# A two-layer encoder: u and v of the mixer as one Strassen product, its last part inside the attention, the engines' order written out

## The chip, the cores and the metric

The kernel runs on one core of one Trainium2 chip. The metric is the device time of one execution in microseconds (us). TensorE (PE) multiplies matrices, VectorE (DVE) and ScalarE (ACT) prepare and finish its operands, GpSimd (POOL) and SyncE (SP) issue transfers.

## What is computed

The input is 512 tokens of 1024 channels, on a grid of 8 rows by 64 columns. Two layers follow each other; then comes a last RMSNorm.

```python
def reference(...):
    for l in range(L):
        x = x + 0.5 * swiglu(rms_norm(x, ffn1_norm[l]), ffn1_w_in[l], ffn1_w_out[l])
        x = x + mixer(rms_norm(x, mix_norm[l]), mix_w_in[l], ...)
        x = x + 0.5 * swiglu(rms_norm(x, ffn2_norm[l]), ffn2_w_in[l], ffn2_w_out[l])
    return rms_norm(x, final_norm)

def mixer(h, w_in, gate_bias, rpb, w_na_out, w_f_out, w_o):
    z = h @ w_in                    # q, k, v, uf: 512 columns each; ga, gf: 1024 each
    y_na = neighbourhood_attention(q, k, v, rpb) @ w_na_out   # 8 heads of 64
    y_f = fourier_mix(uf) @ w_f_out # real part of a 2-D DFT over positions and 128 channels, 4 groups
    return (sigmoid(ga + gate_bias[0]) * y_na + sigmoid(gf + gate_bias[1]) * y_f) @ w_o
```

The change touches the mixer: how v and uf ("u" in the kernel) are computed, and in which order the rest of the mixer stands around that.

## The kernel before

**Numbers in two parts.** Each operand of a product is split into a high part (`fp32r`, made on ACT by a copy) and a low part (the difference, made on DVE). `mm3` (L285 to L288) and `late_low` (L446 to L450) then issue three matmuls: high by high, high by low, low by high. A weight "granule" is 128 by 1024; `Item.prep` makes its `whi` on ACT (L175, or L170 when negated) and its `wlo` on DVE (L178, L171), three buffers of each. `Item.summed` (L160) adds two granules on DVE where a product needs a sum of weights.

**Products in seven parts.** The feed-forward products, the two gates and the last product of the mixer use Strassen's scheme: `product` issues one part of 24 matmuls of 128x512 (four blocks of the inner dimension, two blocks of rows, three matmuls), and seven parts in place of eight give the four quadrants. Sums of activations (the tiles `t1` to `t3`) and of weights go in, `snap` (L517) copies a result out of PSUM, `less` (L522) subtracts. Where `strassen` is called with `dma=True`, sums of weights are made by transfers that accumulate, issued on POOL's queue (L146).

**The mixer's order.** `proj_U` computes u without such a scheme, together with a mirrored copy from activations that `mirrored` (L986, L987) reverses; `proj_V` computes v. Both take all eight blocks of the inner dimension in three matmuls each. After u comes `norm.rstd()`, the reciprocal root on DVE (L304 to L309), and `norm.spread(R)`, which writes it to DRAM and reads it back as a row for all partitions (`row<-r`, `R<-row`, on POOL's queue). Then:

```python
        u = proj_U()
        vt = proj_V()
        bias_for(0)
        ...
        for g in range(4):
            four_pos(g)
        proj_q(0)
        proj_k(0)
        for g in range(4):
            four_ch(g)
        proj_q(1)
```

`four_pos` transforms over positions and rotates, `four_ch` over channels; each of the four groups leaves a pair `y` that `rows_of` multiplies with the Fourier weights later (`fill`). `proj_T` makes one pair of heads of q or k: 24 matmuls, a product with `R` (L970), high and low. `att_scores` (L1104), `att_probs` (maxima with the bias on DVE L1118, exponentials on ACT L1124, reciprocals L1127, scalings on ACT L1131), `att_trans` (transposes on PE L1140, then `p` high and low) and `att_out` follow per pair of blocks; `att_next(hp)` transposes the two blocks of one pair of heads and scores the next two. PSUM has eight banks, handed out in rotation; `slot` has 23 buffers, `tmp` eight.

A scheduler orders the instructions on each engine by priority. Inside `tc.manual_schedule(engines=...)` the named engines keep the order of the program text; before the change this is used at a few places only, none of them in the first part of the mixer.

## Time and profile before

| | |
|---|---|
| median of 3 runs | 1905.67 us (1904.82 to 1905.99) |
| the profiled execution | 1906.04 us, of which its span is 1904.2 |
| granted TensorE clock | 0.999 |
| layer 0's mixer, first product | from 337 us |
| layer 0's gates, first product | from 492 us |

A row of the profile's groups reads: line, engine, operation, output tile <- input tiles, shapes, count | busy us, mean ns of one | idle time of the engine before them and what ended it. In the table of windows each engine has its busy time and count, then come the granted clock, the share of the transfers and GB/s. In the timeline and the chain the first number is the start and the second the length, both in us.

### The profile page before, as it was taken

What the parts mean: (1) busy time and instruction counts of PE and PEld (TensorE: products, weight loads), DVE (VectorE), ACT (ScalarE), POOL (GpSimd) and SP (SyncE); (2) the same over time, 40 slices, a digit from 0 to 9 for tenths busy, and PEclk for the clock granted to TensorE, in tenths of its full rate; (3) what the DMA queues carried; (4) which work ended last, traced back from release to release, by engine and by line L of the source; (5) the groups of instructions that cost most, each with busy time, mean ns of one, the idle gap of its engine ahead of it and who ended that gap; (6) DMA issues with size and microseconds to landing.
All of it is one profiled execution on the core that took longest, in us unless ns stands there. A gap on an engine that the chain in (4) does not pass through costs nothing.

```text
span 1904.2 us, 25091 instructions
## 1 busy us (share of the span) xinstructions
PE 1891.7 (99%) x9189; PEld 1586.8 (83%) x9189; DVE 1602.4 (84%) x2000; ACT 1161.6 (61%) x1676; POOL 160.7 (8%) x198
## 2 busy tenths in 40 slices
PE   9999999999999999999999999999999999999998
PEld 7888888888888888888888888888888888888886
DVE  7877899586889987889997778995769899787899
ACT  6655665468566755566665556663675576555655
POOL 0101010000111010001010100100001101000010
PEclk9999999999999999999999999999999999999999
DMA  8776499323886776649877664992247867766594
GB/s 301 202 207 187 150 249 320 105 84 104 217 218 166 180 195 204 177 152 262 251 185 210 187 180 152 268 339 74 68 130 215 215 170 175 207 177 177 170 275 147
DMA packets 104636, 364.36 MB, mean 191 GB/s; under 512 B 12032, under 2 KB 12160, under 8 KB 104512
## 3 DMA queue, kind: packets, MB, share of 16 engines
q1 hardware_dynamic: 77568, 270.70, 40.1%
q0 software_dynamic: 26800, 92.04, 26.8%
q8 instruction: 72, 1.18, 0.2%
q14 instruction: 52, 0.43, 0.1%
q10 hardware_dynamic: 144, 0.02, 0.0%
HBM read 357.46 MB, written 2.11 MB: 189 GB/s over the span
## 4 chain that ended last, share of the span: by engine, by line
PE 95%; issue 2%; DMA 2%; DVE 1%; ACT 0%; POOL 0%; DVEq 0%; ACTq 0%; POOLq 0%; SPq 0%
PE A L447 9%; PE A L448 9%; PE A L450 9%; PE o L448 7%; PE o L447 7%; PE o L450 7%; PE ps L286 5%; PE ps L288 5%; PE ps L287 5%; PE B L448 4%; PE B L447 4%; PE B L450 4%; PE C L448 2%; PE C L447 2%; PE C L450 2%; PE tr L540 2%
## 5 line engine op out<-in xcount | busy, mean ns | idle before, releaser
L175 ACT ACTIVATE whi<-raw 128x1024 fp32r<-128x1024 f32 (+1 forms) x528 | 546.1, 1037 | 423.4 <-PE A L448 123.2
L178 DVE TENSOR_TENSOR wlo<-raw,whi 128x1024 fp32r<-128x1024 f32 (+1 forms) x528 | 627.3, 1193 | 191.2 <-ACT whi L175 186.5
L146 POOL DMA_DIRECT2D raw<-in_wst_dram x158 | 136.2, 873 | 1440.2 <-DMA raw<-in_wst_dram 674.7
L160 DVE TENSOR_TENSOR raw<-raw,raw 128x1024 f32<-128x1024 f32 (+1 forms) x146 | 172.6, 1191 | 1.2
L448 PE MATMUL A<-whi,xl 128*128 128x512 f32 x384 | 149.5, 389 | 0.0
L447 PE MATMUL A<-whi,xh 128*128 128x512 f32 x384 | 149.4, 389 | 0.0
L450 PE MATMUL A<-wlo,xh 128*128 128x512 f32 x384 | 110.5, 389 | 0.0
L170 ACT ACTIVATE whi<-raw 128x1024 fp32r<-128x1024 f32 (+1 forms) x79 | 81.6, 1036 | 40.2 <-PE A L448 12.4
L171 DVE SCALAR_TENSOR_TENSOR wlo<-raw,whi 128x1024 fp32r<-128x1024 f32 (+1 forms) x79 | 93.1, 1193 | 12.2 <-ACT whi L170 12.2
L633 ACT ACTIVATE th<-sn,rh 128x512 f32<-128x512 f32 x80 | 56.8, 714 | 69.4 <-DVE sn L522 69.4
L517 ACT ACTIVATE sn<-A 128x512 f32<-128x512 f32 x96 | 56.4, 589 | 51.3 <-PE A L450 51.2
L450 PEld LDWEIGHTS A<-wlo,xh 128*128 128x128 f32 x384 | 72.1, 188 | 15.0
L448 PEld LDWEIGHTS A<-whi,xl 128*128 128x128 f32 x384 | 72.1, 188 | 14.8
L447 PEld LDWEIGHTS A<-whi,xh 128*128 128x128 f32 x384 | 72.1, 188 | 14.8
L447 PE MATMUL B<-whi,t1h 128*128 128x512 f32 x192 | 76.2, 397 | 0.0
L447 PE MATMUL A<-whi,t3h 128*128 128x512 f32 x192 | 75.3, 392 | 0.4 <-ACT sn L517 0.4
L447 PE MATMUL C<-whi,xh 128*128 128x512 f32 x192 | 74.9, 390 | 0.0
L447 PE MATMUL A<-whi,t2h 128*128 128x512 f32 x192 | 74.9, 390 | 0.0
L448 PE MATMUL B<-whi,t1l 128*128 128x512 f32 x192 | 74.8, 390 | 0.0
L448 PE MATMUL A<-whi,t3l 128*128 128x512 f32 x192 | 74.8, 390 | 0.0
L448 PE MATMUL C<-whi,xl 128*128 128x512 f32 x192 | 74.7, 389 | 0.0
L448 PE MATMUL A<-whi,t2l 128*128 128x512 f32 x192 | 74.7, 389 | 0.0
(409 smaller groups left out, 4748.2 us busy)
## 6 DMA issues: line engine op xcount, KB each, us to landing
raw<-in_wst_dram SPq DMA_DIRECT2D x466, 512.0 KB, 5.4
raw<-in_wst_dram POOLq DMA_DIRECT2D x162, 512.0 KB, 7.9
raw<-in_wst_dram SPq DMA_DIRECT2D x30, 256.0 KB, 3.9
bm<-in_bias_dram SPq DMA_DIRECT2D x16, 384.0 KB, 6.0
vs<-v SPq DMA_DIRECT2D x12, 256.0 KB, 4.9
x<-in_xin_dram SPq DMA_DIRECT2D x4, 512.0 KB, 10.2
raw<-in_wst_dram POOLq DMA_DIRECT2D x8, 256.0 KB, 8.7
dft<-in_dft_dram POOLq DMA_DIRECT2D x8, 256.0 KB, 6.2
```

The costliest lines, as they stand in the source:

```text
L146: G.dma_start(out=self.t, in_=wst[GRAN_AT[self.plus]][:, 0 : self.n], accum_op=ALU.add)
L160: V.tensor_tensor(self.raw.t, self.raw.t, self.add.t, ALU.add)
L170: S.activation(hi, t, AF.Copy, scale=-1.0)
L171: self.last = V.scalar_tensor_tensor(lo, t, -1.0, hi.bitcast(F32), ALU.mult, ALU.subtract)
L175: S.activation(hi[:, cs], t[:, cs], AF.Copy)
L178: self.last = V.tensor_tensor(lo[:, cs], t[:, cs], hi[:, cs].bitcast(F32), ALU.subtract)
L286: PE.matmul(ps, lh, rh, start=start, stop=False, skip_group_check=again)
L287: PE.matmul(ps, lh, rl, start=False, stop=False, skip_group_check=again)
L288: PE.matmul(ps, ll, rh, start=False, stop=stop, skip_group_check=again)
L447: PE.matmul(ps, lh, rh, start=start, stop=False, skip_group_check=again)
L448: PE.matmul(ps, ll, rh, start=False, stop=False, skip_group_check=again)
L450: PE.matmul(ps, lh, rl, start=False, stop=stop, skip_group_check=again)
```

## The change

- **u and v are one product** (`proj_UV`). Their weights form a block matrix, u's beside v's, and it is multiplied in seven parts, in the order 1, 5, 6, 2, 3, 7, 4. Projections of q and k stand between the parts: their granules come in the weights' order behind the fifth, sixth, second, third and seventh part. u is complete behind part 3. Part 4 is issued behind the first scores.
- **The mirrored u** comes from the finished u: `turn` multiplies its high and low part by a reversed identity (`mir`), four matmuls, inside the second k projection. `flip` now holds the small product that reverses the reciprocal roots.
- **Activations**: the mixer's normalised x is copied raw, then split once per quarter (`quad_high`: 1024 columns high, 1024 low), as its sums (`combos`, shared with the feed-forward stage) are taken from the raw copy. The reciprocal root uses ACT's square root (`rstd_steps`), so ACT loads the table of the square root in the feed-forward stage before, and that of the exponential in the mixer.
- **Fourier stage in two halves**: groups 0 and 1, then 2 and 3 inside the attention. `four_pos`, `four_ch` and `att_probs` are cut into steps (`rotated`, `four_q`, `four_y`, `four_high`; class `Probs` with `maxes`, `exps`, `inverse`, `scaled`; `att_pv`, `att_split`), `proj_T` into the product, high and low.
- **Order written out** for PE, DVE and ACT, from the mixer's start to the scores of the third pair of heads. `tmp` has 11 buffers. The first block of rows of the Fourier product (`pf`) moves there too. In `fill` of `o`, the first two blocks start with three of their four inner blocks.

The core of the diff (cut; lines of the old `proj_U`, `proj_V` and of the plain loop over heads are left out):

```diff
+                for key in (behind or {}).get(m, ()):
+                    add(Raw(key))
...
-            for name, n in (("u", 4), ("v", 4), ("qk", 8), ("f", 4)):
-                for g in range(n):
-                    add(Raw((s, name, g)))
+            qk = [(s, "qk", g) for g in range(8)]
+            strassen(s, lambda q: "u" + q, 0, two, (1, 5, 6, 2, 3, 7, 4), True, behind={5: qk[0:1], 6: qk[1:2], 2: qk[2:3], 3: qk[3:4], 7: qk[4:5]})
+            for key in qk[5:] + [(s, "f", g) for g in range(4)]:
+                add(Raw(key))
...
+        def quad_high(self, i, j):
...
+            S.activation(hq, raw, AF.Copy)
+            return lambda: V.tensor_tensor(lq, raw, hq.bitcast(F32), ALU.subtract)
...
+        def rstd_steps(self):
+            ms, q, t = small("ms", 4), small("sq", 4), small("rt", 4)
+            r = self.r = small("r", 4)
+            V.tensor_tensor(ms, self.ssq[:, 0:4], self.ssq[:, 4:8], ALU.add)
+            V.tensor_scalar(ms, ms, 1.0 / D, EPS, ALU.mult, ALU.add)
+            S.activation(q, ms, AF.Sqrt)
+            yield
+            V.reciprocal(r, q)
+            V.tensor_tensor(t, r, r, ALU.mult)
+            V.scalar_tensor_tensor(t, t, -0.5, ms, ALU.mult, ALU.mult)
+            V.scalar_tensor_tensor(r, t, 1.5, r, ALU.add, ALU.mult)
+            yield
...
+        def combine(m):
+            p, a, b, op = {
+                5: ((0, 0), (0, 0), (0, 1), ALU.subtract),
+                7: ((0, 1), (0, 1), (1, 1), ALU.subtract),
+                6: ((0, 0), (1, 1), (0, 0), ALU.add),
+                4: ((1, 0), (1, 0), (0, 0), ALU.subtract),
+            }[m]
+            V.tensor_tensor(raw[p], raw[a], raw[b], op)
+            yield
+            if m != 4 or not t4:
+                acts[m] = (slot(F32R, f"t{m}h"), slot(F32R, f"t{m}l"), 0)
+            h, l, _ = acts[m]
+            S.activation(h, raw[p], AF.Copy)
+            yield
+            V.tensor_tensor(l, raw[p], h.bitcast(F32), ALU.subtract)
+            yield
+        return acts, combine
...
-            return mp.tile([P, T], dt, tag="tmp", name=nm(s), bufs=8)
+            return mp.tile([P, T], dt, tag="tmp", name=nm(s), bufs=11)
...
+        def proj_UV():
+            acts, combine = combos(norm, None)
+            ws.depth = 8
+            steps = {m: combine(m) for m in (5, 6, 7, 4)}
+            def step(m, n=1):
+                for _ in range(n):
+                    next(steps[m])
+            step(5)
+            def t1():
+                step(5, 2)
+                norm.squares(1, 0)
+            pa = pair("A")
+            product(pa, acts[1], K4, True, hook=t1)
+            root = norm.rstd_steps()
+            next(root)
+            ws.items[ws.prepped + 1].summed()
+            next(root)
+            norm.spread(R)
+            ws.prep(ws.pos + 3)
+            low10 = norm.quad_high(*norm.due.pop(0))
+            s1 = snap(pa)
+            norm.low01()
+            step(6, 2)
+            pb = pair("B")
+            product(pb, acts[5], K4, True, hook=low10)
+            sb = snap(pb)
+            S.activation(small("sq", 1), ones, AF.Exp)
+            step(6)
+            q0 = proj_T(DH**-0.5)
+            step(7, 2)
+            product(pa, acts[6], K4, False, again=True, hook=lambda: step(7))
+            s2 = snap(pa)
+            k0 = proj_T(None)
+            step(4, 2)
+            q0 = q0()
+            step(4)
+            pc = pair("C")
+            product(pc, acts[2], K4, True)
+            q[0] = q0()
+            q1 = proj_T(DH**-0.5)
+            k0 = k0()
+            less(pc, s1)
+            k[0] = k0()
+            product(pb, acts[3], K4, False, again=True)
+            q1 = q1()
+            less(pb, s2)
+            uh, ul = slot(F32R, "uh", (2, T)), slot(F32R, "ul", (2, T))
+            S.activation(uh, s2, AF.Copy)
+            q[1] = q1()
+            norm.flip()
+            V.tensor_tensor(ul, s2, uh.bitcast(F32), ALU.subtract)
+            S.activation(mir, mirror, AF.Copy)
+            flipped = []
+            def turn():
                 for c in range(2):
+                    pm = bank()
+                    PE.matmul(pm, mir, uh[:, 1 - c, :], start=True, stop=False)
+                    PE.matmul(pm, mir, ul[:, 1 - c, :], start=False, stop=True)
+                    t = tmp(s="uf")
+                    S.activation(t, pm, AF.Copy, scale=norm.rflip[:, c : c + 1])
+                    flipped.append(t)
+            k1 = proj_T(None, hook=turn)
             constants()
+            us, ue = [[], []], []
             for c in range(2):
                 for op in (ALU.add, ALU.subtract):
                     w = tmp(s="ue")
+                    V.scalar_tensor_tensor(w, s1[:, c, :], norm.r[:, c : c + 1], flipped[c], ALU.mult, op)
+                    ue.append(high_of(w, "u"))
+                    us[c].append(None)
+            for i, low_of in enumerate(ue):
+                us[i // 2][i % 2] = low_of()
+            product(pa, acts[7], K4, False, again=True, ahead=0)
+            ws.depth = FETCH
+            return us, k1, pa, sb, acts[4]
...
+        with tc.manual_schedule(engines={mybir.EngineType.DVE, mybir.EngineType.Activation}):
+            with tc.manual_schedule(engines={mybir.EngineType.PE}):
+                u, k1, pa, sb, acts4 = proj_UV()
+                fp = [four_pos(0), four_pos(1)]
+                bias_for(0)
+                k1 = k1()
+                ws.prep(ws.pos + 2)
+                bt = [rotated(fp[0])]
+                bh = [high_of(bt[0], "b")]
+                bt.append(rotated(fp[1]))
+                bh.append(high_of(bt[1], "b"))
+                less(pa, sb)
+                for c in range(2):
+                    v_high(2 + c, sb[:, c, :])
+                k[1] = k1()
+                b_ = [bh[0](), bh[1]()]
+                q2 = proj_T(DH**-0.5)
+                q2 = q2()
+                p0, p1 = [Probs(i, att_scores(i)) for i in range(2)]
+                p0.maxes(0)
+                p0.maxes(1)
+                p0.exps(0)
+                p1.maxes(0)
+                p0.inverse(0)
+                p0.exps(1)
+                p1.maxes(1)
+                p0.inverse(1)
+                p1.exps(0)
+                product(pa, acts4, K4, False, again=True, ahead=0)
+                ws.prep(ws.pos + 1)
+                q[2] = q2()
+                for c in range(2):
+                    v_high(c, pa[c])
+                f0, f1 = four_ch(b_[0]), four_ch(b_[1])
+                g0, g1 = four_q(f0[1]), four_q(f1[1])
+                for c in range(4):
+                    v_low(c, sb[:, c - 2, :] if c > 1 else pa[c])
+                vs = []
+                for s in range(3):
+                    t = slot(F32R, "vs", (2, T))
+                    nc.sync.dma_start(out=t[0:64].bitcast(F32), in_=vt[s][64:128].bitcast(F32))
+                    nc.sync.dma_start(out=t[64:128].bitcast(F32), in_=vt[s + 1][0:64].bitcast(F32))
+                    vs.append(t)
+                bias_for(1)
+                p1.exps(1)
+                fp = [four_pos(2), four_pos(3)]
+                y0 = four_y(f0[0], g0)
+                p1.inverse(0)
+                y1 = four_y(f1[0], g1)
+                p1.inverse(1)
+                ws.prep(ws.pos + 2)
+                k2 = proj_T(None, 1)
+                y0 = four_high(y0)
+                y1 = four_high(y1)
+                p0.scaled(0)
+                p0.scaled(1)
+                bt = [rotated(fp[0])]
+                bh = [high_of(bt[0], "b")]
+                p1.scaled(0)
+                bt.append(rotated(fp[1]))
+                bh.append(high_of(bt[1], "b"))
+                p1.scaled(1)
+                b_ = [bh[0](), bh[1]()]
+                k2 = k2()
+                ws.prep(ws.pos + 2)
+                fq = []
+
+                def second():
+                    fq.extend([four_ch(b_[0]), four_ch(b_[1])])
+
+                q3 = proj_T(DH**-0.5, 0, hook=second)
+                (f0, f1) = fq
+                g0, g1 = four_q(f0[1]), four_q(f1[1])
+                w0 = four_y(f0[0], g0)
+                w1 = four_y(f1[0], g1)
+                w0 = four_high(w0)
+                w1 = four_high(w1)
+                yf += [y0(), y1()]
+                q3 = q3()
+                ts = transposed(p0.s) + transposed(p1.s)
+                ph = [high_of(t, "p") for t in ts]
+                ph = [h() for h in ph]
+                pt_ = {0: ph[0:2], 1: ph[2:4]}
+                p2, p3 = [Probs(i, att_scores(i)) for i in (2, 3)]
+                k3 = proj_T(None, 0)
+                p2.maxes(0)
+                p2.maxes(1)
+                ws.prep(ws.pos + 1)
+                p2.exps(0)
+                p2.exps(1)
+                p3.maxes(0)
+                p2.inverse(0)
+                p3.maxes(1)
+                p2.inverse(1)
+                yf += [w0(), w1()]
+                p2.scaled(0)
+                p2.scaled(1)
+                p3.exps(0)
+                ws.prep(ws.pos + 2)
+                p3.exps(1)
+                k[2] = k2()
+                q[3] = q3()
+                p3.inverse(0)
+                k3 = k3()
+                p3.inverse(1)
+                bias_for(2)
+                vch = {i: (t[:, 0, :], t[:, 1, :]) for i, t in ((0, vt[0]), (1, vs[0]), (2, vt[1]), (3, vs[1]), (4, vt[2]), (5, vs[2]), (6, vt[3]))}
+                o.append(hilo("o"))
+                po = [att_pv(i, pt_.pop(i)) for i in range(2)]
+                first_f.extend([ws.next(0), ws.next(0)])
+                pf = rows_of(yf, 0, first_f)
+                att_split(0, po[0])
+                p3.scaled(0)
+                p3.scaled(1)
+                ts = transposed(p2.s) + transposed(p3.s)
+                k[3] = k3()
+                ph = [high_of(t, "p") for t in ts[0:2]]
+                pt_[2] = [h() for h in ph]
+                att_split(1, po[1])
+                ph = [high_of(t, "p") for t in ts[2:4]]
+                pt_[3] = [h() for h in ph]
+                ps = [att_scores(i) for i in (4, 5)]
+        sc = {i: att_probs(i, z) for i, z in zip((4, 5), ps)}
```

320 lines of the change are left out of this document (150 added, 170 removed).

## The prediction

> **What bounds the kernel now.** I read the page's busy times first, then TensorE's waits, the chain of work that ended last, and the windows over layer 0's mixer (337 to 500 us).
>
> ```profile
> span 1904.2 us, 25091 instructions
> PE 1891.7 (99%) x9189; PEld 1586.8 (83%) x9189; DVE 1602.4 (84%) x2000; ACT 1161.6 (61%) x1676; POOL 160.7 (8%) x198
> ...
> PE ps L132 <- ACT warm L129: 2.7, 1, 2.7
> PE A L447 <- ACT sn L517: 0.4, 2, 0.2
> ```
>
> TensorE (PE) is bound by its own work: in 1904.2 us it waits 3.1 us, 2.7 of them for the warm-up. So a matmul taken away is worth its pitch, as long as everything that feeds PE arrives in time. The pitch is in the chain (start, length, instructions) and in the timeline:
>
> ```profile
> 340.55 0.68 PE ps L288 x3
> 342.60 0.87 PE tr L364 x8
> 382.19 0.12 PE ps L286
> 421.23 1.69 PE L1104 MATMUL ps<-q,q 64*128 64x256 f32 x24
> ```
>
> A 128x512 matmul costs 0.68/3 = 0.227 us, a 128x128 transpose 0.109, a 256-wide matmul of the Fourier stage 0.12, a score matmul on 64 rows (they run in pairs) 1.69/24 = 0.07. (The mean of one, 0.39 us, overlaps its neighbours.)
>
> ```profile
> 337.00:359.60 22.60, 22.60 (x105) 18.82 (x104) 10.96 (x32) 8.70 (x18) 4.55 (x8) 1.00 0.41 134
> 359.60:381.40 21.80, 21.80 (x98) 18.07 (x98) 10.96 (x15) 9.50 (x13) 0.00 (x0) 1.00 0.06 21
> 381.40:400.00 18.60, 18.60 (x112) 16.63 (x112) 16.83 (x30) 8.00 (x12) 0.00 (x0) 1.00 0.53 142
> 400.00:420.00 20.00, 20.00 (x114) 16.69 (x113) 14.81 (x47) 14.46 (x37) 0.00 (x0) 1.00 0.21 67
> 420.00:440.00 20.00, 20.00 (x146) 17.56 (x146) 15.33 (x39) 16.15 (x42) 0.00 (x0) 1.00 0.13 40
> 440.00:460.00 20.00, 20.00 (x128) 17.19 (x125) 13.93 (x49) 15.15 (x44) 0.00 (x0) 1.00 0.15 54
> ```
>
> The columns are PE, weight loads, VectorE (DVE), ScalarE (ACT), POOL, the granted clock (1.00 throughout) and DMA. While u and v are projected, DVE is half idle (10.96 of 22.60); in the attention both feeders have a quarter to a third in reserve (13.93 to 15.33 and 14.46 to 16.15 of 20). That reserve is what this change spends.
>
> **What it removes and adds on PE.**
>
> ```profile
> L286 PE MATMUL ps<-whi,xh 128*128 128x512 f32 x96 | 37.7, 393 | 0.0
> L286 PE MATMUL ps<-whi,flip 128*128 128x512 f32 x32 | 12.4, 389 | 0.0
> ```
>
> u and v are one of three such rows each: 3 x (96 + 32) = 384 matmuls in two layers. Seven parts of 24 are 168 a layer, 336; the mirror of u adds 4 a layer. Net 384 - 336 - 8 = 40 fewer, 40 x 0.227 = **-9.1 us**, or 4.5 a layer. Attention, projections, Fourier and gates keep their counts. Were PE as dense as now, that would be the result: 1906.0 - 9.1 = 1896.9 for a profiled run.
>
> **What it adds on the feeders.** Counting instructions in the two orders, DVE gains, over both layers, 42 operations of 1024 columns (12 weight lows, 4 sums of weights, 8 combinations of activations with their 8 lows, 10 lows of x and u) and twelve subtractions of 512; it loses 32 small lows and 16 flips. By the rows below, and 0.62 us for 512 columns (further down), that is 42 x 1.22 + 12 x 0.62 - 32 x 0.48 - 16 x 0.29 = +39 us of DVE work, all in the mixer. ACT gains weight highs and four table loads.
>
> ```profile
> L178 DVE TENSOR_TENSOR wlo<-raw,whi 128x1024 fp32r<-128x1024 f32 x500 | 609.0, 1222 | 191.0 <-ACT whi L175 186.3 <-DMA raw<-in_wst_dram 2.5
> L296 DVE SCALAR_TENSOR_TENSOR xl<-tr,gn,xh 128x256 fp32r<-128x256 f32 x32 | 14.1, 478 | 0.5 <-ACT xh L295 0.2
> L987 DVE CAST flip<-xl 128x256 fp32r<-128x256 f32 x16 | 4.4, 288 | 0.0
> L175 ACT ACTIVATE whi<-raw 128x1024 fp32r<-128x1024 f32 x500 | 528.6, 1060 | 418.7 <-PE A L448 123.2 <-PE o L448 54.6 <-DVE raw L160 44.9
> L295 ACT ACTIVATE q<-q 128x512 fp32r<-128x512 f32 x8 | 5.1, 633 | 1.1 <-DVE q L970 1.1
> L292 ACT ACTIVATE o<-ps 64x256 fp32r<-64x256 f32 x32 | 10.8, 372 | 4.5 <-PE ps L288 3.8 <-DVE o L293 0.4
> ```
>
> A third of that sits where DVE was half idle, but the written order puts the fourth part, all four v lows, the second Fourier half and two rounds of attention into one stretch. That stretch decides; I add up each engine's queue in it, from layer 0's first `four_ch` to the transposes of the fourth score block (`p3`).
>
> **The stretch, step by step.** PE's own work in it: 84 matmuls of 512 columns x 0.227 = 19.0, 72 of 256 x 0.12 = 8.6, 24 score matmuls x 0.07 = 1.7, 32 transposes x 0.109 = 3.5; together 32.8 us. For DVE and ACT the timeline gives what instructions cost back to back:
>
> ```profile
> 309.00 1.22 DVE L178 TENSOR_TENSOR wlo<-raw,whi 128x1024 fp32r<-128x1024 f32 x1
> 310.14 1.28 DVE L659 SCALAR_TENSOR_TENSOR x<-o,x 128x512 f32<-128x512 f32 x2
> 410.15 0.42 DVE L1118 CUSTOM_DVE_ANT_0 s<-ps,bm 128x256 f32<-128x256 f32 x1
> 410.50 0.42 DVE L1118 CUSTOM_DVE_ANT_0 s<-ps,bm 128x256 f32<-128x256 f32 x1
> 411.33 0.49 ACT L1124 ACTIVATE s<-s,nmx 128x256 f32<-128x256 f32 x1
> 411.82 0.50 ACT L1124 ACTIVATE s<-s,nmx 128x256 f32<-128x256 f32 x1
> 412.32 1.70 ACT L1131 ACTIVATE s<-s,rs 128x256 f32<-128x256 f32 x4
> 421.49 2.05 ACT L292 ACTIVATE p<-ps 128x512 fp32r<-128x512 f32 x4
> 422.10 2.48 DVE L293 TENSOR_TENSOR p<-ps,p 128x512 fp32r<-128x512 f32 x4
> ```
>
> - DVE: 5 weight lows x 1.14 = 5.7; 16 score maxima x 0.35 = 5.5; 25 of 512 columns (lows of q, y, p, v, b, the R products, the rotations) x 0.62 = 15.5; 12 of 256 x 0.35 = 4.2; 15 small ones, 1.2. Sum 32.1 us, 98% of PE's 32.8.
> - ACT: 16 exponentials x 0.49 = 7.9; 16 scalings x 0.42 = 6.8; 6 weight highs x 1.06 = 6.4; 4 p highs, 2.1; 10 highs of q, y, b x 0.6 = 6; v, fq and o highs, 3. Sum 32 us, 97%.
>
> Both would fit if neither ever waited for the other, but each executes in the written order, and the order alternates between them. DVE is held at these heads of its queue: the low of a k2 weight, whose high ACT reaches only behind six exponentials (they start one maximum after DVE: 0.35 + 6 x 0.49 + 1.06, less eight maxima 8 x 0.35, 1.6 us); the next weight's low, whose high is behind q's high (0.63 + 1.06 = 1.7); the p lows behind q's high (0.63 + 0.51 = 1.1); the low of the first y weight, its high behind scalings and exponentials (1.7); reciprocals, 0.3. Together 6.4 us. DVE starts the stretch 1.9 us ahead of PE, since the second low of the fourth part is due 1.8 us before that product ends. After its last product ahead of `p3`'s scalings, there follow one weight low 1.14, the highs of k and o (0.63 + 0.37, with an o low of 0.42 between), four scalings 1.7, and half of the transposes: 4.5 us. So PE leaves the stretch after 32.1 + 6.4 - 1.9 + 4.5 = 41.1 us for 32.8 of work: **8.3 us late**.
>
> On PE this shows in pieces: k2's projection waits for a bank that `fq`'s copy on ACT frees (1.4), the second `four_ch` for b's low (1.3), a score block for a bank that the q product on DVE frees (1.1), k3 and `rows_of` for lows (1.4), the transposes of `p3` for its scalings (3.2).
>
> Elsewhere: k0's projection waits 0.75 us, as its low is queued behind the combination for part 7 and the high behind t7's; the fourth part 0.2, its second weight's high standing behind the v highs. For the rest (parts 1 to 3 and 5 to 7, the mirror, the second half of the attention, the gates) I find each operand ready before PE arrives, with 0.3 us (u's low) to 6 us in hand, so these edits cost nothing while that holds. In all 8.3 + 0.95 = 9.25 us a layer, 18.5 for two.
>
> The forecast: 1906.04 - 9.1 + 18.5 = 1915.4 for a profiled run (its span 1904.2 plus 1.84 around it); the median of the runs is 0.37 below that execution, so **1915.1 us**. The stall's lower bound is all heads free: 32.1 + 4.5 - 1.9 = 34.7, 1.9 a layer, and nothing where the tail overlaps. Its upper bound is as many heads again that I took for covered, 9.25 + 6.4 = 15.7 a layer. I stay at the sum, because each head is a named wait.
>
> **A table rule.** The change adds a square root and an exponential's set per layer, two loads each.
>
> ```profile
> 1786.36 0.62 ACT L170 ACTIVATE whi<-raw 128x512 fp32r<-128x512 f32 x1
> 1786.99 1.28 ACT L813 ACT_TABLE_LOAD   x1
> 1788.28 0.20 ACT L813 ACTIVATE sq<-ones 128x1 f32<-128x1 f32 x1
> ```
>
> The load starts where the instruction before it ends and the next starts where it ends: 1.28 us and nothing more. Both new loads lie where ACT has idle time before PE needs it, so I cost them at nothing; without that cover, 4 x 1.28 = 5.1. The Trainium skill, page "ScalarE: Activation LUTs", section "What ACT_TABLE_LOAD costs", adds a drain of about 1.38 us to the 1.28 at every switch. By it (an estimate from that page) up to 5.5 us more would have to be hidden, and the sum could reach 1920.6; the trace shows no such drain, so it is left out.
>
> **The rivals.**
>
> *The feeders keep up.* DVE's heads of queue are free because ACT runs ahead: the windows show it idle for a fifth to a quarter of the attention even now. Then PE loses 0 to 2.5 us a layer, and the time is 1896.6 to 1901.6, faster. It decides from a stall under 4.5 us a layer; against it speaks that DVE's 32.1 us leave 0.7 in 32.8. Chance 0.24.
>
> *A draw.* Half of the named heads are covered: 2.6 to 6.4 us a layer, 1902 to 1909.5. Chance 0.14.
>
> *The loads come late.* The R row goes through POOL's queue, and the accumulating loads stand behind it:
>
> ```profile
> row<-r POOLq DMA_DIRECT2D x5, 2.0 KB, 11.3
> R<-row POOLq DMA_DIRECT2D x5, 256.0 KB, 6.3
> raw<-in_wst_dram POOLq DMA_DIRECT2D x162, 512.0 KB, 7.9
> ```
>
> R takes 11.3 + 6.3 = 17.6 us after the reciprocal root; four products of 24 x 0.227 = 5.4 lie between, 21.8, so 4 us are in hand, and 1 to 4 for the accumulated weights. Were the loads 5 us later, each layer would lose up to 4 more: 1923. Chance 0.04.
>
> *The clock drops.* PE's clock is 1.00 in every window; stalls of 1 to 3 us are new. If after each stall PE ran at half clock for as long as the stall lasted, 8.3 us a layer would do 4.2 of work: 8.3 more for two layers, 1923.4. The Trainium skill, "TensorE: Matmul & The Clock Gate", section "HAM oscillation — how this bites in real kernels", warns of idle gaps over some 3.4 us; no run here shows one, and the longest I sum is 3.2. Chance 0.03.
>
> **The numbers.** The stalls as summed, with 6.4 to 12 us a layer (1909.5 to 1920.6), have the remaining 0.55. A measurement of this kernel tells 0.2%, 3.8 us, from no change: faster 0.24, same 0.14, slower 0.62. The range for 8 in 10 leaves out about a tenth at each end: 1898 to 1921.5; the likeliest case's own is 1909.5 to 1920.6.
>
> **What would show it.** In the changed kernel's waits PE should have some 21 us instead of 3.1, nearly all between `four_ch` and the `p3` transposes, released by ACT's scalings and `fq` and by DVE's lows of weights and b. DVE should be busy over 90% there. PE's waits under 6 us would disprove the stalls; waits in the first products, on R or on loads, would mean I put them in the wrong place; a matmul pitch above 0.227 would bring in the clock.

## The result and the profile after

The changed kernel takes 1924.39 us (median of 4 runs, 1922.61 to 1926.9) where the kernel before takes 1905.83 in the same comparison: a ratio of 1.0099, 95% interval [1.0082, 1.0117]. It is slower, as forecast, but by 18.6 us, twice the 9.4 forecast, and above the range's upper end of 1921.5.

The profiled execution took 1926.9 us. Its page, the busy times:

```profile
span 1923.7 us, 25086 instructions
PE 1894.6 (98%) x9149; PEld 1583.0 (82%) x9149; DVE 1639.2 (85%) x1992; ACT 1193.4 (62%) x1714; POOL 171.5 (9%) x210
```

PE has the 40 matmuls fewer (9149 for 9189), and 19.5 us more of span. What it waits for (total, times, longest):

```profile
PE A L469 <- ACT sn L539: 2.8, 2, 1.9
PE ps L135 <- ACT warm L132: 2.7, 1, 2.7
PE ps L1212 <- DVE q L1013: 2.7, 2, 1.4
PE ps L293 <- ACT fq L1168: 2.5, 2, 1.3
PE ps L294 <- DVE b L1037: 2.2, 2, 1.1
PE ps L293 <- DVE p L1037: 1.8, 2, 1.0
PE tr L374 <- DVE x L1699: 1.6, 1, 1.6
PE ps L295 <- DVE wlo L181: 0.9, 2, 0.5
PE ps L1264 <- ACT s L1245: 0.8, 2, 0.4
PE o L470 <- DVE c4l L300: 0.6, 1, 0.6
```

Line by line these are k2's bank behind `fq` (1.3 a layer; forecast 1.4), the second `four_ch` on b's low (1.1; 1.3), a score block's bank behind the q product (1.4; 1.1), k3 on the p lows (1.0), k0's low at the mixer's start (0.5; 0.75). Three lines were not forecast: the gate's third part (`A <- sn`), the update of `x`, and `c4l` in the last feed-forward stage. One is far too small: `p3`'s transposes (L1264) wait 0.8 us in layer 0 and nothing in layer 1, not 3.2 a layer.

The windows over layer 0's attention (PE, weight loads, DVE, ACT, POOL, granted clock, DMA) show where PE loses and a thing that the kernel before did not have:

```profile
402.00:422.00 20.00, 18.72 (x116) 15.75 (x115) 14.58 (x42) 12.52 (x31) 0.00 (x0) 1.00 0.40 112
422.00:442.00 20.00, 16.65 (x94) 13.65 (x93) 16.91 (x47) 13.63 (x31) 0.00 (x0) 0.91 0.18 36
442.00:462.00 20.00, 18.98 (x124) 16.00 (x123) 13.25 (x38) 17.15 (x49) 0.00 (x0) 1.00 0.19 65
521.00:531.00 10.00, 8.06 (x29) 6.14 (x28) 8.22 (x8) 5.51 (x6) 0.86 (x1) 0.83 0.97 259
436.00:440.00 4.00, 3.96 (x11) 3.13 (x12) 4.00 (x12) 3.51 (x11) 0.00 (x0) 0.58 0.02 4
```

The granted clock falls to 0.58 just behind two stalls in a row, and again behind the gate's. In PE's timeline one matmul there starts 0.43 us after the other (start, length, last idle time and its releaser):

```profile
434.08 0.97 PE L1212 MATMUL ps<-q,q 64*128 64x256 f32 x11 [1.25 <-DVE q L1013]
436.04 0.47 PE L293 MATMUL ps<-xh,whi 128*128 128x512 f32 x1 [0.99 <-DVE p L1037]
...
437.40 0.63 PE L294 MATMUL ps<-xl,whi 128*128 128x512 f32 x1
437.83 0.63 PE L295 MATMUL ps<-xh,wlo 128*128 128x512 f32 x1
```

Eight matmuls at 0.427 instead of 0.227 us here, eleven in layer 1, eight behind the gate: 27 x 0.2 = 5.4 us.

By stages, from the starts of matmuls in the timelines. "Mixer" runs from the last piece of the feed-forward stage ahead of it to the gate's first matmul, "gates" from there to the third part of the mixer's last product (`wC`), and the last row from that mark in layer 1 to the last matmul; without any stall the new mixer would take 166.51 - 20 x 0.227 = 161.98 us. A small table with the executions that are discussed below:

| us | before | changed | changed, again | ACT free (e5) | DVE, ACT free (e1) | rewritten (e7) |
|---|---|---|---|---|---|---|
| mixer, layer 0 | 166.51 | 172.91 | 173.46 | 163.42 | 163.26 | 164.50 |
| mixer, layer 1 | 166.51 | 173.23 | 173.16 | 164.29 | 163.60 | 164.69 |
| gates, layer 0 | 102.11 | 105.54 | 103.33 | 103.51 | 101.83 | 101.72 |
| gates, layer 1 | 102.13 | 102.78 | 105.51 | 102.74 | 102.78 | 101.72 |
| last feed-forward stage | 355.95 | 358.35 | 355.82 | 355.69 | 355.98 | 355.64 |

So a changed mixer loses 10.9 to 11.5 us a layer against its own work.

### The profile page after: what moved, and what is told of

It is laid out like the page before. It is cut to its first block, busy times and chain, and to the rows that moved or that the text cites. A ratio compares the mean times of both kernels' runs of the same rounds, so it can differ in the third digit from the quotient of the medians.

```text
span 1923.7 us, 25086 instructions
## 1 busy us (share of the span) xinstructions
PE 1894.6 (98%) x9149; PEld 1583.0 (82%) x9149; DVE 1639.2 (85%) x1992; ACT 1193.4 (62%) x1714; POOL 171.5 (9%) x210
## 4 chain that ended last, share of the span: by engine, by line
PE 80%; DVE 7%; DMA 5%; issue 4%; ACT 4%; POOL 0%; SPq 0%; DVEq 0%; ACTq 0%; POOLq 0%
PE A L469 9%; PE A L470 9%; PE A L472 9%; PE o L472 6%; PE o L470 6%; PE o L469 5%; PE B L469 5%; PE B L470 5%; PE B L472 5%; DMA raw<-in_wst_dram 4%; PE C L470 2%; PE C L469 2%; PE C L472 2%; DVE wlo L181 2%; PE ps L295 2%
## 5 line engine op out<-in xcount | busy, mean ns | idle before, releaser
L181 DVE TENSOR_TENSOR wlo<-raw,whi 128x1024 fp32r<-128x1024 f32 (+1 forms) x536 | 638.0, 1197 | 185.5 <-ACT whi L178 184.4
L178 ACT ACTIVATE whi<-raw 128x1024 fp32r<-128x1024 f32 (+1 forms) x536 | 553.1, 1037 | 387.7 <-PE A L470 127.8
L149 POOL DMA_DIRECT2D raw<-in_wst_dram x166 | 144.4, 896 | 1412.8 <-DMA raw<-in_wst_dram 740.8
L173 ACT ACTIVATE whi<-raw 128x1024 fp32r<-128x1024 f32 (+1 forms) x83 | 85.8, 1036 | 40.6 <-PE o L470 12.8
L470 PE MATMUL C<-whi,xl 128*128 128x512 f32 x208 | 81.0, 389 | 0.0
L470 PE MATMUL B<-whi,xl 128*128 128x512 f32 x208 | 81.0, 389 | 0.0
L469 PE MATMUL B<-whi,xh 128*128 128x512 f32 x208 | 80.9, 389 | 0.0
L472 PE MATMUL C<-wlo,xh 128*128 128x512 f32 x208 | 59.8, 389 | 0.0
L472 PE MATMUL B<-wlo,xh 128*128 128x512 f32 x208 | 59.8, 389 | 0.0
L293 PE MATMUL ps<-xh,whi 128*128 128x512 f32 x128 | 52.3, 409 | 4.3 <-ACT fq L1168 2.5
L469 PE MATMUL B<-whi,t5h 128*128 128x512 f32 x136 | 54.2, 399 | 0.0
```

What stands on the lines that cost most here:

```text
L149: G.dma_start(out=self.t, in_=wst[GRAN_AT[self.plus]][:, 0 : self.n], accum_op=ALU.add)
L173: S.activation(hi, t, AF.Copy, scale=-1.0)
L178: S.activation(hi[:, cs], t[:, cs], AF.Copy)
L181: self.last = V.tensor_tensor(lo[:, cs], t[:, cs], hi[:, cs].bitcast(F32), ALU.subtract)
L293: PE.matmul(ps, lh, rh, start=start, stop=False, skip_group_check=again)
L469: PE.matmul(ps, lh, rh, start=start, stop=False, skip_group_check=again)
```

## The experiments

**e1: is it the order or the volume?** VectorE's and ScalarE's order in the mixer's block is handed back to the scheduler; TensorE's stays written out.

```diff
-        with tc.manual_schedule(engines={mybir.EngineType.DVE, mybir.EngineType.Activation}):
+        with ExitStack():
             with tc.manual_schedule(engines={mybir.EngineType.PE}):
```

> The changed kernel with one line undone: in the block that holds the seven parts and the first half of the attention, TensorE's order stays written out, but VectorE's and ScalarE's is left to the scheduler again. Same operations, same count, same loads. Theory (heads of queue): the 9 us a layer that TensorE loses there come from VectorE and ScalarE waiting for each other in the written order, not from their volume. Then the stalls between the first channel product and the transposes of p3 fall from some 9 us a layer to under 1.5, the granted clock stays at 1.00 there, and the time falls from 1924.4 by about 19 us of stalls and 4.3 us of clock to 1900 us (1896 to 1906), below the kernel before at 1905.8. The stall of the gate's third part (2.1 us, layer 0) stays. Rival (volume): VectorE has 32.1 us of work against TensorE's 32.8 there, and no order fits it in: at least 5 us a layer stay, 1912 us or more. Rival (loads and room): the stalls come from weight loads or from buffers that come free late, which an order does not change: 1920 us or more.

Measured 1904.48 us (11 runs, 1899.72 to 1907.48), ratio to the kernel before 0.9995 [0.9986, 1.0003]. The three PE waits that are left:

```profile
PE ps L135 <- ACT warm L132: 2.7, 1, 2.7
PE A L469 <- ACT sn L539: 0.8, 1, 0.8
PE ps L1212 <- DVE p L1037: 0.6, 2, 0.3
```

Every stall of the stretch is gone or at most 0.3 us: one line took 9.7 and 9.6 us off the two mixers. Volume, loads and buffers are out as causes of these stalls. The expected 1900 was nearly that of the profiled execution (1899.72, the fastest); the median is 4.5 higher, still within the range given. e6 comes back to that.

**e5: which engine's order?** Only ScalarE's is handed back.

```diff
-        with tc.manual_schedule(engines={mybir.EngineType.DVE, mybir.EngineType.Activation}):
+        with tc.manual_schedule(engines={mybir.EngineType.DVE}):
```

> The changed kernel with ScalarE's order alone left to the scheduler in the mixer's block; VectorE's stays as it is written out, and so does TensorE's. Theory (heads): each stall there begins with a low on VectorE whose high stands too far back in ScalarE's written order, behind exponentials, scalings or other highs. Then ScalarE's order alone is enough: stalls between the first channel product and the transposes of p3 under 2 us a layer, clock 1.00 there, and 1899 to 1907 us, as with both orders left free (1904.5). Rival (VectorE's own order): the lows stand in the wrong order on VectorE itself, or its 32.1 us are too many; then most of the 9 us a layer stay, 1915 us or more.

Measured 1901.58 us (7 runs, 1898.69 to 1905.93), ratio 0.9979 [0.9968, 0.9989]: 23 us off by ScalarE's order alone. What DVE waits for between 404 and 454 us in the changed kernel:

```profile
DVE wlo L181 <- ACT whi L178: 7.9, 4, 2.8
DVE p L1037 <- ACT p L1034: 2.4, 2, 1.2
DVE rs L1240 <- ACT s L1237: 0.7, 1, 0.7
```

and ACT's and DVE's busy time in the same stretch with ACT free, to be held against the windows above:

```profile
402.00:422.00 20.00, 20.00 (x120) 17.37 (x119) 17.57 (x49) 16.41 (x40) 0.00 (x0) 1.00 0.57 145
422.00:442.00 20.00, 20.00 (x140) 17.59 (x141) 17.88 (x47) 17.09 (x42) 0.00 (x0) 1.00 0.20 67
```

Four weight lows wait for highs that stand too far back in ScalarE's queue; with that order free no weight low waits there, ACT does 33.5 us of work in 40 instead of 26.2, and PE is never idle in these windows. DVE's written order does no harm once ACT's is free.

**e2 and e3: why does the gate's third part wait?** e2 puts one statement back where the kernel before has it; e3 gives the kernel before the room of the changed one.

```diff
# e2, on the changed kernel        # e3, on the kernel before
         next(first)               +        mir = mp.tile([P, P], F32R, tag="mir", ...)
-        f_some(1)                 +        S.activation(mir, mirror, AF.Copy)
         att_outs(3)               -            return mp.tile([P, T], dt, tag="tmp", ..., bufs=8)
         t12, _ = next(first)      +            return mp.tile([P, T], dt, tag="tmp", ..., bufs=11)
         ws.prep(ws.pos + 2)
+        f_some(1)
```

> The changed kernel with one statement moved back to where the kernel before had it: the row product of f behind the first negative weights at the end of the mixer (row product after the weight's preparation instead of ahead of the last attention outputs). Theory (order at the tail): the gate's third part waits 2.1 us in layer 0 and 1.0 us in layer 1 because VectorE comes to the gate's activations some 1.9 us later than before and the loads behind them are issued late. Moved back, the stall falls to under 0.6 us, and with it go the 9 matmuls at double pitch behind it (1.8 us): 1924.4 becomes 1919 to 1922 us, with up to 1 us of small new stalls in the last attention outputs. Rival (room): the raw buffers of the next stage lie over the mixer's larger pool and the loads wait for that; then nothing changes, 1923 to 1926 us, and the stall stays at 2.1.

> The kernel before with the changed kernel's room in the mixer's pool and nothing else: eleven instead of eight buffers for temporary tiles, and the mirror's tile with its one copy. Theory (order at the tail): room alone does not make the gate's weights late; the stall of the gate's third part stays at 0.5 us or less and the time at 1905.8 us (1904.5 to 1908). Rival (room): the loads of the gate's weights start late because their buffers lie over other tiles of the mixer; the third part stalls by some 2 us a layer, with the clock's loss behind it 1908 to 1913 us.

e3 took 1905.93 us, ratio 0.9999 [0.999, 1.0008]: room costs nothing. In e2 the stall at the gate is gone. ACT's timeline shows the weight's high, first in the changed kernel, then in e2:

```profile
522.77 1.06 ACT L178 ACTIVATE whi<-raw 128x1024 fp32r<-128x1024 f32 x1 [2.43 <-DMA raw<-in_wst_dram]
523.73 0.58 ACT L539 ACTIVATE sn<-A 128x512 f32<-128x512 f32 x1
```

```profile
522.27 1.06 ACT L178 ACTIVATE whi<-raw 128x1024 fp32r<-128x1024 f32 x1 [0.31 <-PE A L470]
523.24 0.58 ACT L539 ACTIVATE sn<-A 128x512 f32<-128x512 f32 x1
```

In the changed kernel the bank's copy `sn`, which PE needs, stands behind a high whose load is late; in e2 the load is there, and the gates take 101.8 and 101.7 us. The load is one that accumulates, and POOL issues it only behind a weight low on DVE; again the changed kernel, then e2:

```profile
514.80 0.85 POOL L183 DMA_DIRECT2D raw<-in_wst_dram  x1 [11.72 <-DVE wlo L181]
```

```profile
514.25 0.85 POOL L183 DMA_DIRECT2D raw<-in_wst_dram  x1 [10.03 <-DVE wlo L181]
```

The gate's first matmul is at 499.09 and 500.77 us, so this issue comes 15.7 us behind it in the changed kernel and 13.5 in e2, and the load takes 7.9 and 7.7 us from there: DVE's lateness of 2.2 us is the load's. The other executions agree: with the statement moved back (e6, e7, e10) no gate waits, with it in its new place (e1, e5, e11) five of six do, for 0.8 to 1.9 us. But e2's time is 1923.34 us (ratio 1.0092 [1.0078, 1.0106]), not to be told from the changed kernel's, for its mixers are 1.9 and 3.3 us longer: the last attention outputs wait (0.88 and 0.62 us a layer, in place of 0.40), and `p3`'s transposes wait 2.0 us in both layers, which e11 explains. The theory on the stall holds, the forecast of its worth does not.

**e4: stalls of set length, first try.** PE is held by chains of settings on GpSimd in the feed-forward products.

```diff
+        for n in HOLDS[held[1]]:
+            PE.matmul(ps[:, 0:2], mirror, held[0][:, 0:2], start=True, stop=True)
+            for _ in range(n):
+                G.memset(held[0], 0.0)
+            for _ in range(2):
+                PE.matmul(ps[:, 0:256], mirror, held[0][:, 0:256], start=True, stop=True)
```

> The kernel before with TensorE held up on purpose at 16 places in its feed-forward products: a tiny matmul on a tile waits for a chain of 1 to 8 settings of that tile on GpSimd, then two 256-wide matmuls run. Some places have two or three such holds in a row (1 and 1, 2 and 2, 2 and 1, 3 and 1, 1 and 1 and 1, 3 and 3 links). Asked is which idle time is followed by matmuls at double pitch (0.43 instead of 0.227 us), and for how long. In the changed kernel single stalls of 1.27, 1.44 and 1.74 us were followed by none, 1.40 and 1.15 us in a row by some 3 us of it, 1.68 and 1.10 by some 5 us, and 2.1 us alone by some 3 us. Theory (idle time within a few us): it is the sum of idle time in a short stretch that counts, the limit lies between 1.74 and 2.1 us, and pairs and triples above it count like single holds. Rival (single gap): only one gap over a limit counts, pairs of short ones do not; the pair in the changed kernel was then something else. Rival (every stall): the clock halves for as long as the stall was, whatever its length: then also a stall of 1 us is followed by 1 us of double pitch. Rival (long gaps alone): by the Trainium skill, TensorE: Matmul & The Clock Gate, section HAM oscillation, only idle gaps over some 3.4 us bring the clock down; then holds under 3.4 us are followed by none.

It answers nothing. PE waited 0.7 us in two holds of the many, since the scheduler put other products' matmuls between the two sides of each hold. A stall needs an order that is written out.

**e8 and e9: stalls of set length, with PE's order fixed.** The same hold, in e1's kernel ahead of parts 5, 2, 3, 7 and the projections of k2 and k3; e9 has holds in pairs and threes. (e8's holds write over some columns of sums that parts 3 and 7 add to, so it computes other values; in e9 they have a bank of their own.)

```diff
+    HOLDS = (2, 3, 4, 5, 6, 8, 4, 5, 6, 7, 3, 10)                                           # e8
+    HOLDS = ((), (3, 2), (4, 3), (2, 2, 2), (6,), (7,), (3, 3), (5,), (4, 2), (3, 2), (7,), (3, 2))  # e9
```

> The version with VectorE's and ScalarE's order left free, in which TensorE's order stays written out, and so a hold does hold TensorE: at six places of each layer's mixer (ahead of parts 5, 2, 3 and 7 and of k2's and k3's projection) a matmul of two columns on a tile is followed by 2, 3, 4, 5, 6, 8 (first layer) and 4, 5, 6, 7, 3, 10 (second) settings of that tile on GpSimd and a matmul that waits for the last of them. The length of each stall is read from the run, some 1 to 4 us. Theory (idle time within a few us): stalls under 1.7 us are followed by no double pitch (0.43 instead of 0.227 us), those over 2.1 us by some 3 us of it, and those between may go either way, since 1.40 and 1.15 us in a row were followed by it in one execution and not in another; the double pitch comes some 1 us after the stall. Rival (every stall): the clock halves after each stall for as long as it was. Rival (long gaps alone): nothing up to 3.4 us, by the gap that the Trainium skill, TensorE: Matmul & The Clock Gate, section HAM oscillation, warns of.

> As the run with fixed holds (there single stalls of 0.98, 1.41, 1.77, 1.78, 2.14 and 2.51 us were followed by no double pitch, 2.88, 3.25, 3.98 and 9.12 us by 1.2, 2.4, 2.0 and 2.4 us of loss), now with holds in pairs and threes, some 0.6 us of work between them, into a bank of their own: 3 and 2 settings of the tile (1.41 + 0.98 us) at three places, 4 and 3 (1.77 + 1.41), 2 and 2 and 2 (3 x 0.98), 3 and 3 (2 x 1.41), 4 and 2 (1.77 + 0.98), and alone 6 (2.51), 7 (2.88, twice) and 5 (2.14). Theory (sum within a few us): what counts is the idle time within some 3 us, so pairs of 2.7 us and more are followed by double pitch though neither stall is, those of 2.4 us mostly not, and a single 2.88 is again. Rival (single gap): only one gap over some 2.6 us counts; no pair is followed by it, and the pair of 1.40 and 1.15 us in the changed kernel must have had another cause.

Stalls are start to start beyond the usual pitch; the loss is what the matmuls behind them take beyond 0.227 each. (The 9.12 and 4.73 us are no holds: a projection waits there for a weight's low. The gates' own stalls are not in the table.)

| stall, us | loss behind it, us |
|---|---|
| alone: 0.98, 1.41 (twice), 1.77, 1.78, 2.14 (twice), 2.51 (three times) | none |
| alone: 2.14, 7 us behind another stall of 4.73 | 1.6 |
| alone: 2.88 (three times) | 1.2, 1.2, 1.6 |
| alone: 3.25, 3.98, 4.73, 9.12 | 2.4, 2.2, 1.4, 2.4 |
| 1.35 + 1.04; 1.77 + 1.04 | none |
| 1.41 + 1.04 (twice) | 1.5, 1.5 |
| 1.41 + 1.41; 1.77 + 1.41; 1.04 + 1.04 + 1.04 | 0.8, 1.4, 2.4 |

Windows of 3.41 us over some of them (clock in the column behind POOL; why this length is said below): alone 2.14 (two lines) and alone 3.25 us (two lines) in e8,

```profile
403.39:406.80 3.41, 2.08 (x11) 1.68 (x9) 3.18 (x5) 3.08 (x6) 1.04 (x4) 1.00 0.00 0
406.80:410.22 3.42, 2.79 (x13) 2.39 (x14) 3.42 (x6) 1.76 (x4) 0.52 (x2) 1.00 0.00 0
451.17:454.59 3.42, 1.13 (x16) 0.91 (x14) 3.42 (x11) 1.53 (x5) 1.87 (x6) 1.00 0.00 0
454.59:458.00 3.41, 2.63 (x7) 2.25 (x8) 2.36 (x13) 3.41 (x13) 0.62 (x2) 0.50 0.41 104
```

and in e9 three of 1.04 us (two lines) and 1.77 + 1.04 (two lines):

```profile
396.26:399.67 3.41, 1.47 (x11) 1.21 (x9) 3.41 (x6) 2.53 (x4) 1.35 (x5) 1.00 0.00 0
399.67:403.08 3.41, 2.78 (x8) 2.30 (x9) 2.47 (x4) 0.63 (x1) 0.52 (x2) 0.50 0.11 22
1355.40:1358.82 3.42, 1.83 (x12) 1.51 (x11) 1.88 (x3) 1.58 (x2) 1.24 (x4) 1.00 0.00 0
1358.82:1362.23 3.41, 2.55 (x15) 2.14 (x14) 0.64 (x2) 0.00 (x0) 1.73 (x4) 1.00 0.24 59
```

What counts is idle time in sum, not one gap: three stalls of 1 us do what one of 3.25 does, and one of 2.51 does nothing. By their length alone it goes either way between 2.0 and 2.9 us: a gate's stall of 2.00 us in e9 had a drop behind it, 1.77 + 1.04 had none.

When the clock changes says more. In each execution its changes lie whole multiples of 3.41 us apart (in the changed kernel it falls at 436.61, 525.36 and 1388.93 us, 26 and 253 times 3.413 apart), and it stays at half for one such stretch or two, behind the 9.12 us for three. The windows above are cut at these marks. Cut so over ten executions (the changed kernel twice, e1, e2 and e5 to e10; where no drop gives the marks, the fall behind the last matmul does), all 21 stretches at full clock with 1.7 us or more of PE's idle time in them are followed by half clock; of those with less, which reach 1.64 us, a single one is (1.42 us, layer 1 of the changed kernel). So a stall counts by what of it falls into one stretch: the 2.14 us lie in two, 1.33 and 0.63, as do 1.77 + 1.04 (1.59 and 0.86); of the 3.25 us 2.3 lie in one, of the three of 1.04 1.9.

The clock is down before the last stall ends (from 454.59 us on, for a stall that ends at 455.37), and the loss is 0.8 to 2.4 us whatever the stall: 9.12 us cost no more than 3.25. So "as long as the stall" falls, and so does "long gaps alone". The Trainium skill, TensorE: Matmul & The Clock Gate, section HAM oscillation — how this bites in real kernels, gives its abstract rule as no idle gaps over some 3.4 us; here 2.88 us alone and three of 1.04 were enough, and the measurement decides. The Trainium skill, TensorE: Matmul & The Clock Gate, section What's actually happening, has a free-running window watch the activity; that sums count and that equal stalls end differently agrees with it.

**e11: what recurs?** The changed kernel once more, unaltered.

> The changed kernel once more, unaltered, for a second profiled execution: which of its losses recur. Theory: the stalls between the first channel product and the transposes of p3 recur to a tenth of a us (some 8 to 9 us a layer with those at the mixer's start), since they come from the written order; whether the clock drops after the pair of 1.40 and 1.15 us, and the waits on late loads (the gate's third part 2.1 and 1.0 us, the update of x 1.7 us), differ from execution to execution. Rival: all of it recurs, the clock's drops at the same places too. Time 1921 to 1927 us either way.

Measured 1920.69 us (4 runs, 1919.09 to 1924.87), ratio 1.0074 [1.0059, 1.0089]. The lines of the stretch recur to 0.2 us, except that of `p3`'s transposes (the second line here), 0.8 in the first execution; the first line is the gate's, outside the stretch:

```profile
PE A L469 <- ACT sn L539: 3.3, 2, 1.9
PE ps L1264 <- ACT s L1245: 3.2, 4, 2.0
```

The reason is the clock. In layer 0 the same pair of stalls (1.37 and 1.15 us) was followed by no double pitch this time; `p3`'s transposes then waited 2.0 us, and the drop came there. Windows cut at the clock's marks, first the pair of stalls in the first execution, then the pair and the transposes in this one:

```profile
433.20:436.61 3.41, 1.54 (x14) 1.28 (x15) 2.23 (x5) 2.55 (x6) 0.00 (x0) 1.00 0.00 0
436.61:440.03 3.42, 3.42 (x10) 2.65 (x9) 3.42 (x11) 2.93 (x10) 0.00 (x0) 0.50 0.02 5
```

```profile
430.71:434.12 3.41, 2.64 (x28) 2.27 (x26) 3.31 (x12) 1.26 (x2) 0.00 (x0) 1.00 0.00 0
434.12:437.54 3.42, 1.98 (x16) 1.64 (x17) 2.24 (x5) 2.99 (x6) 0.00 (x0) 1.00 0.00 0
447.78:451.19 3.41, 1.40 (x11) 0.96 (x9) 2.93 (x6) 2.25 (x6) 0.00 (x0) 1.00 0.47 153
451.19:454.60 3.41, 3.05 (x21) 2.69 (x22) 1.80 (x4) 2.45 (x6) 0.00 (x0) 0.50 0.01 4
```

The pair's idle time, 1.9 us in one stretch of the first execution, is split into 0.8 and 1.4 in this one; which it is depends on where the marks happen to lie. In the first execution PE lost 1.6 us to the clock at 437, ACT caught up meanwhile, and the transposes waited 0.8 us, in two waits, at a clock of 1.00. The six mixers of three executions agree: behind a drop of 6.83 us the transposes waited 0.0 us (layer 1, first execution), behind one of 3.41 us 0.8 (layer 0 there, layer 1 here), and with no drop ahead of them 2.4 (layer 0 here, both layers of e2). So a drop ahead of a stall with the same cause is given back by that stall. The gate's wait recurs with other lengths (1.5 and 2.1 us, for 2.1 and 1.0); the update of `x` does not wait.

**e6 and e10: the tail's order on top.**

```diff
-        f_some(1)
         att_outs(3)
         t12, _ = next(first)
         ws.prep(ws.pos + 2)
+        f_some(1)
```

> Both edits: VectorE's and ScalarE's order in the mixer's block left to the scheduler, and the row product of f at the mixer's end moved back behind the first negative weights. With the orders free alone the time was 1904.5 us where the sum of work and stalls gave 1900; its profiled execution has one stall of 1.0 us on the gate's third part left, and the sum of the work is 1896.9. Theory (order at the tail): that wait is near its limit and longer in other executions than in the profiled one; moved back it is gone for some 0.7 us of new waits: 1899 to 1903 us. Rival: what keeps the time at 1904.5 is not this wait; then 1903 to 1906 us.

> The version with ScalarE's order alone left to the scheduler, with the row product at the mixer's end moved back too. Expected, if the wait on the gate's third part (1.7 and 0.9 us in the profiled execution) is worth what it lasts: 1901.6 - 2.6 + 1.3 of new waits in the last attention outputs and their weight's low = 1900 us (1898.5 to 1902). Rival (given back): the new waits and the later rows take all of it, as with both orders left free, where the same step changed nothing (1904.5 and 1904.3): 1901 to 1903 us.

e6: 1904.32 us (ratio 0.9991 [0.9982, 1.0]); e10: 1901.14 us (11 runs, ratio 0.9977 [0.9968, 0.9986]). Each is within 0.5 us of the version without the step, so e6's theory fails and its rival stands, while e10's time lies in both of its ranges: what the gates gain, 0.1 to 1.8 us a layer, the last attention outputs and waits elsewhere take (part 2 in e6, `c4l` in the last feed-forward stage in both). In both pairs the version with DVE's order written out is 3 us faster, though the intervals of the ratios just overlap, and DVE's waits at layer 0's start differ; first e6, then e5:

```profile
DVE q L1013 <- DMA R<-row: 8.2, 1, 8.2
```

```profile
DVE wlo L181 <- ACT whi L178: 7.1, 6, 1.6
```

Left to the scheduler, DVE has the q product, which needs the R row, ahead of two weight lows. The scheduler also puts other work between DVE's steps of the reciprocal root, the last of which starts 3.6 us behind the reciprocal (0.6 in e5), and so R lands at 365.0 us in e1 and 366.7 in e6, against 361.8 in e5. In e6 part 2 waited 1.7 us, in layer 0 of e1's profiled run not at all. The written order puts three weight lows ahead of the product. That the 3 us come from this is argued from these executions, not shown; and the runs of e5, which has no such wait, spread as widely (7.2 us) as those of e1 (7.8).

**e7: another written order.** All three engines stay written out, with separate steps for highs and lows, and the tail's row product is moved back as in e2 (cut):

```diff
+                ws.high()
+                v_high(0, pa[0])
+                f0 = four_ch(b0_)
+                q[2] = q2l_()
                 ...
+                ws.low()
+                v_high(1, pa[1])
+                p1.maxes(1)
```

> The changed kernel with the orders of all three engines still written out in the mixer's block, but another one: weight highs and lows, q's and k's product, high and low are separate steps, each high stands on ScalarE ahead of the exponentials or scalings that it stood behind, each low on VectorE only after its high can be done, and the p rounds follow each other more closely; with the row product at the mixer's end moved back too. Same operations, same counts. Theory (heads): the loss was in this one order, not in writing an order out; sums of row durations give no stall over 0.3 us in the stretch and 0.7 us at the mixer's start: 1896.9 + 2 x 1.5 = 1900 us (1897 to 1904). Rival (a written order cannot follow the chip): small differences of each execution from the rows accumulate, and a fixed order waits where the scheduler's does too: 1905 to 1912 us. Rival (volume): 1912 us or more.

Measured 1901.76 us (8 runs, 1900.46 to 1904.27), ratio 0.9979 [0.9969, 0.9989]. No PE wait inside the stretch is left, no drop of the clock; 1900 was forecast. The loss was in this one order, not in writing an order out.

## Why the prediction was right and wrong

- **Fewer matmuls, 9.1 us:** right in the count; the best versions (1901.1 to 1901.8) come within 5 us of the 1896.9 that it gives without any stall.
- **The heads of the queues:** right in kind and place, and near in sum. DVE waits where it was said, for highs in ScalarE's queue: the named heads of 1.6, 1.7, 1.1 and 1.7 us are 1.8, 1.7, 1.2 and 1.8 in layer 0, and freeing that queue alone removes the stalls (e5). In layer 0 the stalls over 0.15 us, start to start, sum to 8.1 us in the first execution and 9.3 in the second; 9.25 were forecast. The lower bound, all heads free, was 1.9 a layer: e1 and e5 measure 1.3 to 2.3. The 3.2 us at `p3`'s transposes are 2.0 and a second wait of 0.4 where no drop comes ahead of them. That all of PE's waits sum to 19.7 us, near the 21 forecast, is luck in part: only some 10 of them lie in the stretch, and the gates, the update of `x` and `c4l` (5.0 in all) stand in for what `p3` did not wait.
- **DVE over 90% busy there:** wrong, and by its own numbers: 32.1 us of work in 41.1 is 78%; the windows have 44.7 of 60. The reserve of both feeders before, read there as a quarter to a third, is 19 to 30% by the rows shown.
- **"The rest costs nothing" failed:** the gates were named among what keeps its cover, with 0.3 us or more in hand. One row product moved ahead of the gate's first sums makes DVE 2.2 us later, and with it the issue of an accumulating load; the third part waits 1.0 to 2.1 us (e2; e3 excludes the room), with a drop behind the longer ones. The prediction has no term for loads that DVE's lateness delays there.
- **The clock rival failed in size and form.** It had 0.03 and half clock for as long as the stall. Stalls of 1.1 to 2 us in a row reach the limit by their sum, and the change made several. The term was put at nothing; in the profiled execution it is 5.4 us (27 matmuls), 3.8 in the mixers and 1.6 at a gate, less what `p3`'s transposes gave back.
- **The sum for the profiled execution,** 1926.9 against 1915.4: mixers +3.7 (22.2 for 18.5; the clock, less what `p3` gave back), gates +4.1, last feed-forward stage +2.4 (the update of `x` 1.6, `c4l` 0.6; both missing from the second execution), time around the span 3.2 instead of 1.84, +1.3; the other stages -0.1. Together 11.4 of 11.5. In e11's execution of the same kernel (1924.87 us) the parts of the mixers and the gates recur, +4.2 and +4.6, that of the last stage does not. Both profiled executions are the slowest of their four; e11's median, 1920.69, is 5.6 us over the forecast and inside the range, where the first median is 9.3 over.
- **The rivals:** "the feeders keep up" is what the same operations do in another order (e5, e7: 1901.6 and 1901.8, its own upper end); the written order decided against it. Late loads took part at the gates, not at R (in e6, with DVE's order free, at R too). The table rule's drain is again not there: the new load takes its 1.28 us and nothing more.

```profile
351.67 1.06 ACT L539 ACTIVATE sn<-B 128x512 f32<-128x512 f32 x2
352.74 1.28 ACT L1083 ACT_TABLE_LOAD   x1
354.03 0.20 ACT L1083 ACTIVATE sq<-ones 128x1 f32<-128x1 f32 x1
```

## What to carry to other kernels

An order written out on two engines that feed each other is a set of head-of-queue waits: add up each engine's queue up to every high whose low the other engine needs next, and try each engine's order free by itself before writing both. Short stalls that lie close together must be added, since the clock goes by their sum; a stall far from others and under some 1.7 us cost its own length only here. And a stall taken away ahead of another one with the same cause may give nothing, as the next one grows by it.

## What was not expected of the hardware

The granted clock changes only at marks 3.41 us apart. It halves behind a stretch between two marks that holds 1.7 us or more of idle time, in one stall or in three (21 of 21; one more at 1.42), for one or two stretches (three behind the 9.12 us), and the loss, 0.8 to 2.4 us in e8 and e9, does not grow with the stall (9.12 us cost 2.4). Equal stalls of 1.4 + 1.15 us had a drop behind them in one execution and none in the next, as the marks cut them differently. Without a drop PE resumes at full pitch: after a stall of 2.51 us the matmuls are 0.23 us apart from the fourth one on.
